# The last hidden pair of a Strassen MLP: its squared features stored raw and split later on POOL, first bank copies on VectorE

## The chip, the cores and the metric

The kernel runs on one NeuronCore of one Trainium2 chip. The metric is the device time of one execution in microseconds (us). TensorE (PE) multiplies; VectorE (DVE), ScalarE (ACT) and GpSimd (POOL) do the elementwise work; SyncE (SP) issues nearly all DMAs. SBUF is the on-chip memory, PSUM holds matmul results in eight banks of 128 partitions x 512 fp32, DRAM is off chip.

## What is computed

One layer of a diffusion backbone on 1024 latent tokens and 128 context tokens. Time mixing comes first (two thirds of the time); the change is in the MLP behind it:

```python
x = x + gate1 * rms_norm(y, lp['g_post_mix'])
h = rms_norm(x, lp['g_pre_mlp']) * (1.0 + scale2) + shift2
f = jnp.square(jax.nn.relu(jnp.einsum('btd,df->btf', h, lp['w_mlp1'])))   # 1024 -> 4096
f = jnp.einsum('btf,fd->btd', f, lp['w_mlp2'])                            # 4096 -> 1024
x = x + gate2 * rms_norm(f, lp['g_post_mlp'])
```

## The kernel before

Every fp32 operand of a matmul is split into a high and a low part (type F32R): ScalarE copies to the rounded type (high), VectorE or POOL subtracts that from the original (low). A product is three matmuls: high-high, high-low, low-high.

**First MLP matmul.** The 4096 hidden columns are 16 pairs p of 2 x 128. For p >= 2, `strassen(p, hooks)` (L2210) does a pair with Strassen's scheme, in eleven steps; after step s it calls the functions in `hooks[s]`, so these lists place all other work. `store` (L2112) puts the squared features in SBUF: `ft[0]` and `ft[1]`, one for each 128 hidden columns, hold 512 tokens in `[:, 0]`, 512 in `[:, 1]` and the last 128 in `[:, 2, 384:512]`. The second matmul uses Strassen too, with A11, A12, A21, A22 as the four 128x512 blocks of a pair. It needs seven split operands of a pair, A11, A12, A22 and the sums S1 to S4: `f_sum` (L2130) makes a sum on VectorE, `f_split` (L2138) splits one operand (one ScalarE copy, one VectorE subtraction, one store of 512 KB to the DRAM tensor `Fd[p]`), `c_split` (L2146) does the 128 last tokens (`Fc[p]`). A pair's operands are made during the next pair; the last pair (p = 15) has no next one, so its splits stand in a row behind `strassen`, ahead of the second matmul (the loop over `("A11", "S1", ...)`).

**Second MLP matmul.** `mlp2(g, hooks)` (L2384) runs for g = 0 to 7; group g covers pairs 2g and 2g + 1 (e = 0, 1). Group 7 is the only one that reads pair 15. A group starts with a context step for each half h of the output columns (banks `ps_s`, `ps_P`), then four passes u over `QUAD`, each of seven steps of six matmuls (`STEP2`): steps 0, 2, 4 and 6 share one bank (`ps_g`), step 1 has `ps_m`, steps 3 and 5 share `ps_G`. After each step `take` (L2346) brings the bank to the accumulator `acc` in SBUF, because the next step on the same bank needs it read first. In group 0 the two context takes and four of a pass's seven (steps 0, 2, 3 and 6, the first to reach their part of `acc`) copy the bank on ScalarE (L2348); all others add on VectorE (L2350).

**What surrounds it.** `f_load(g, u)` (L2330) loads a pass's split operands, 896 KB for each e, into the tiles `f` (`FT2`, four of them, u mod 2 by e), two passes ahead; `c_load` loads the context's. `group_hooks(g)` (L2420) lists, by (pass, step), the work for group g + 1: `w_load`/`w_half` load the W2 rows, `w_t` (L2311) makes the Strassen sums T1, T2, T4, T3 of W2 on POOL, `w_s` (L2317 copy on ScalarE, L2318 subtraction on POOL) splits B11 to B22 and the Ts. For group 0 the same is done on VectorE in the hooks of the last pair. The order is written by hand: each engine runs its instructions in the order in which the code emits them, and SP issues its DMAs so too, each waiting for its semaphores.

## Time and profile before

| | us |
|---|---|
| median of 3 runs | 1717.57 (1716.85 to 1719.27) |
| the profiled execution, its own time | 1720.59 |
| its span, first to last instruction | 1718.8 |
| PE busy in the span | 1586.3 (92%) |
| DVE, ACT, POOL busy | 1110.8, 803.7, 516.9 |

The profiled execution is 3.0 us above the median of the runs, and 1.8 us of it lie outside the span. The mean granted TensorE clock is 0.973 of full speed. In the rows below, a line of a timeline has start and duration (us), engine, line, operation, out<-in, the count, and in brackets the engine's idle time before it and what ended it. A line of busy time by stage has the stage, its length, then busy us and (xcount) of PE, PEld, DVE, ACT and POOL, the granted clock, the DMA engines' share and GB/s. A line of instructions by form has busy us and mean ns, and behind the bar the idle time before them. The stretch that the change touches begins with the last pair, at about 1299 us of the span, and ends with the groups of the second matmul.

### The profile page before, as it was taken

Reading aid. Unit: us, or ns where it says so; the run is one execution under the profiler, and the core shown is the slowest. Engines: PE = TensorE matmul, PEld = TensorE weight load, DVE = VectorE, ACT = ScalarE, POOL = GpSimd, SP = SyncE. Lnnn points to the kernel's source line nnn. Section 1 sums busy time; section 2 is a strip of 40 time slices with the busy share of each in tenths; the row PEclk is TensorE's granted clock in tenths of the full one; section 3 lists DMA queues with packets and bytes.
Section 4 is the critical chain, followed back from the end, with each engine's and each line's share of the span. In section 5 each row is a group of like instructions: output and inputs, shape, how many; then the busy total and the mean of one; then the engine's idle time right before and its main releaser. Section 6 shows DMA issues by size and latency. Waiting matters only on the chain.

```text
span 1718.8 us, 33152 instructions
## 1 busy us (share of the span) xinstructions
PE 1586.3 (92%) x13035; PEld 1337.5 (78%) x13035; DVE 1110.8 (65%) x1884; ACT 803.7 (47%) x1549; POOL 516.9 (30%) x593
## 2 busy tenths in 40 slices
PE   6799988898998999779998999999999699999996
PEld 2678777777887776657686999999999578888884
DVE  2835676576876887956648986677667334444458
ACT  3734443343425577635445666666666422222112
POOL 3100186758310210111220000000000387666635
PEclk9899999989999999989999999999999899999999
DMA  9544857674753767899943467766667755566667
GB/s 312 190 135 132 205 139 185 158 193 113 186 128 95 177 138 182 200 215 253 244 171 122 143 203 236 232 224 220 222 221 261 279 194 215 223 232 233 226 242 260
DMA packets 362556, 341.19 MB, mean 199 GB/s; under 512 B 104600, under 2 KB 322912, under 8 KB 362400
## 3 DMA queue, kind: packets, MB, share of 16 engines
q1 hardware_dynamic: 360288, 331.53, 63.8%
q0 software_dynamic: 2112, 7.55, 1.3%
q8 instruction: 102, 1.67, 0.4%
q14 instruction: 54, 0.44, 0.1%
HBM read 214.72 MB, written 124.29 MB: 197 GB/s over the span
## 4 chain that ended last, share of the span: by engine, by line
PE 63%; DVE 13%; DMA 9%; POOL 5%; ACT 4%; issue 3%; SPq 3%; DVEq 0%; POOLq 0%; ACTq 0%
PE ps_g L2405 9%; PE ps_g L2221 6%; PE ps_P L2221 6%; PE ps_G L2405 4%; PE ps_g L531 3%; PE ps_G L2221 3%; PE ps_g L532 3%; PE ps_g L533 3%; PE ps_g L1662 3%; PE ps_m L2405 2%; POOL ar L1028 2%; POOL ar L1024 2%; PE ps_m L2221 2%; PE ps_G L1503 2%; PE ps_m L1534 2%
## 5 line engine op out<-in xcount | busy, mean ns | idle before, releaser
L531 PE MATMUL ps_g<-hH,wH 128*128 128x384 f32 x552 | 209.5, 380 | 2.6 <-DVE hH L270 1.9
L532 PE MATMUL ps_g<-hL,wH 128*128 128x384 f32 x552 | 191.5, 347 | 6.4 <-DVE hL L484 6.2
L533 PE MATMUL ps_g<-hH,wL 128*128 128x384 f32 x552 | 190.3, 345 | 0.0
L2318 POOL TENSOR_TENSOR sL<-w2r,sL 128x512 fp32r<-128x512 f32 x8 | 10.4, 1305 | 451.5 <-ACT sL L2317 449.4
L2350 DVE TENSOR_TENSOR acc<-ps_g,acc 128x512 f32<-128x512 f32 x116 | 80.0, 691 | 94.1 <-PE ps_g L2405 76.6
L531 PEld LDWEIGHTS ps_g<-hH,wH 128*128 128x128 f32 x552 | 107.9, 196 | 18.0 <-issue 8.5
L2221 PE MATMUL ps_P<-h2H,ws 128*128 128x384 f32 x432 | 118.3, 334 | 0.0
L532 PEld LDWEIGHTS ps_g<-hL,wH 128*128 128x128 f32 x552 | 108.0, 196 | 10.5 <-DVE hL L484 9.1
L2405 PE MATMUL ps_g<-sH,fT 128*128 128x512 f32 x408 | 109.1, 399 | 2.2 <-DVE acc L2350 1.3
L533 PEld LDWEIGHTS ps_g<-hH,wL 128*128 128x128 f32 x552 | 107.6, 195 | 0.0
L2405 PEld LDWEIGHTS ps_g<-sH,fT 128*128 128x128 f32 x408 | 77.2, 190 | 22.4 <-DVE acc L2350 2.6
L1024 POOL TENSOR_TENSOR ar<-ar 128x252 f32<-128x252 f32 (+22 forms) x124 | 79.6, 642 | 44.0 <-DMA ar<-NAd 35.3
L2120 ACT ACTIVATE ft<-ft 128x384 f32<-128x384 f32 x138 | 72.4, 524 | 40.8 <-DVE ft L2119 37.8
L1028 POOL TENSOR_TENSOR ar<-ar 128x252 f32<-128x252 f32 (+22 forms) x124 | 87.5, 705 | 9.3
L2221 PEld LDWEIGHTS ps_P<-h2H,ws 128*128 128x128 f32 x432 | 78.8, 188 | 0.0
L2405 PE MATMUL ps_G<-sL,fT 128*128 128x512 f32 x252 | 70.7, 403 | 3.0 <-ACT acc L2348 2.9
L1539 DVE TENSOR_TENSOR SV<-ps_m,Dt 64x256 f32<-64x256 f32 x136 | 57.1, 421 | 23.6 <-PE ps_m L1534 20.7
L2221 PE MATMUL ps_P<-h2L,ws 128*128 128x384 f32 x216 | 72.2, 334 | 0.0
L2350 DVE TENSOR_TENSOR acc<-ps_G,acc 128x512 f32<-128x512 f32 x60 | 41.4, 690 | 38.0 <-PE ps_G L2405 38.0
L2317 ACT ACTIVATE sL<-tt 128x512 fp32r<-128x512 f32 x31 | 19.6, 632 | 96.0 <-POOL tt L2311 64.7
L2221 PE MATMUL ps_G<-oT,ws 128*128 128x384 f32 x336 | 63.9, 339 | 0.2 <-DVE ft L2119 0.2
L1503 PE MATMUL ps_G<-SV,r 128*32 128x64 f32 x1152 | 53.7, 228 | 10.7 <-DVE SV L1539 10.3
(526 smaller groups left out, 4175.1 us busy)
## 6 DMA issues: line engine op xcount, KB each, us to landing
fT<-Fd SPq DMA_DIRECT2D x64, 896.0 KB
Fd<-fs SPq DMA_DIRECT2D x108, 512.0 KB
KGd<-ar SPq DMA_DIRECT2D x96, 192.0 KB
r<-KGd SPq DMA_DIRECT2D x36, 512.0 KB
mw<-in_w_mod_dram SPq DMA_DIRECT2D x64, 256.0 KB
w1r<-in_w_mlp_dram SPq DMA_DIRECT2D x32, 512.0 KB
w2r<-in_w_mlp_dram SPq DMA_DIRECT2D x31, 512.0 KB
raw<-in_w_in_dram SPq DMA_DIRECT2D x26, 512.0 KB
```

The lines of the kernel that those rows point to most:

```text
L531: T.matmul(ps, wH[:, k, :], hH[b][:, k, :], start=(k == 0), stop=False)
L532: T.matmul(ps, wH[:, k, :], hL[b][:, k, :], start=False, stop=False)
L533: T.matmul(ps, wL[:, k, :], hH[b][:, k, :], start=False, stop=(k == 7))
L1024: E.tensor_tensor(out=t, in0=X[:, :, 0:m, j:j + 1].to_broadcast([128, 2, m, w]), in1=n[:, :, j % 8:j % 8 + 1, j + 1:32].to_broadcast([128, ...
L1028: E.tensor_tensor(out=X[:, :, 0:m, j + 1:32], in0=X[:, :, 0:m, j + 1:32], in1=t, op=ALU.subtract)
L1503: T.matmul(RU[n][r0:r0 + 32, 0, p, :], KRG[n][kq][:, e, p, kc, 0:32], SV[n][s % NSV][:, e, p, :], start=True, stop=True)
L1539: Q.add("V", cv(256), lambda e=e, ks=ks: V.tensor_tensor(out=SV[n][(s + 1) % NSV][ks, e], in0=x["S"][ks], in1=dv[ks], op=ALU.mult), r=[("S ...
L1662: T.matmul(z["ps"], y["t"][:, q // 2, k], wo_t[4 + k][q % 2][:, hs_], start=first, stop=last and stop)
L2120: S_ = lambda: [S.activation(out=f, in_=x, func=fn) for x, fn in ((src if add is None else f, AF.Relu), (f, AF.Square))]
L2221: T.matmul(ps[ch], w[:, qw, k], h[q][:, k, :], start=(new and k == n == 0), stop=(k == 3 and n == 2), skip_group_check=True)
L2350: V.tensor_tensor(out=acc_(i, h), in0=ps, in1=acc_(i, h), op=ALU.add)
L2405: T.matmul(ps[ch], f[:, OPI[fx], qf], w[:, qw], start=(new and e == n == 0), stop=(e == 1 and n == 2), skip_group_check=True)
```

## The change

Four things change.

1. The last pair's operands are no longer made behind `strassen`. Its four blocks and the two 128-column remainders go raw to new DRAM tensors `Ar`, `Cr` (six stores, 1152 KB in place of 3840 KB).
2. `later()` makes the operands during groups 1 to 4 (the table allows up to 5): raw blocks are loaded into three tiles `lr`, POOL makes the four sums, and 14 half operands (128x256) and two context tiles are split by a ScalarE copy and a POOL subtraction in the unused end of the `f` tiles (now 12 slots long, 9 before), then stored to `Fd[15]` and `Fc[15]`. `plan()` gives one piece to each of the eight places of `ROOM` in a group, with its store and loads two places later.
3. `take` copies on VectorE where it copied on ScalarE.
4. `f_load(0, 1)` is issued in two parts inside the last pair (hooks 8 and 10), and group 0's `w_load(1, 1)` moves into its hooks at (0, 0).

```diff
+    Ar = [[dr.tile([128, 512], F32, name=f"Ar{i}{b}") for b in range(2)] for i in range(2)]
+    Cr = [dr.tile([128, 128], F32, name=f"Cr{i}") for i in range(2)]
...
+    def raw(i, b):
+        SY.dma_start(out=Ar[i][b][:], in_=ft[i][:, b])
+
+    def later():
+        l0, l1, l2 = lr
+        rooms = itertools.cycle(range(4))
+        P = NP - 1
+        ld = lambda t, x: lambda: SY.dma_start(out=t, in_=Ar[int(x[2]) - 1][int(x[1]) - 1][:])
+        sums = lambda t, x, y, op: lambda: G.tensor_tensor(out=t, in0=x, in1=y, op=op)
+
+        def half(t, x, h):
+            def fn():
+                r = FT2[divmod(next(rooms), 2)][:, 9:11]
+                f = t[:, 256 * h:256 * h + 256].rearrange("p (u c) -> p u c", c=128)
+                S.activation(out=r[:, :, 0], in_=f, func=AF.Copy)
+                G.tensor_tensor(out=r[:, :, 1], in0=f, in1=r[:, :, 0].bitcast(F32), op=ALU.subtract)
+                return lambda: SY.dma_start(out=Fd[P][:, 2 * h:2 * h + 2, OPI[x]].bitcast(F32), in_=r.bitcast(F32))
+            return fn
...
+        return [(None, [ld(l0, "A21"), ld(l1, "A22"), ld(l2, "A11")]),
+                (half(l1, "A22", 0), []), (half(l1, "A22", 1), []), (sums(l0, l0, l1, ALU.add), [ld(l1, "A12")]),
+                (half(l0, "S1", 0), []), (half(l0, "S1", 1), []), (half(l2, "A11", 0), []), (half(l2, "A11", 1), []),
+                (sums(l0, l0, l2, ALU.subtract), []), (half(l0, "S2", 0), []), (half(l0, "S2", 1), []),
+                (half(l1, "A12", 0), []), (half(l1, "A12", 1), []), (sums(l0, l1, l0, ALU.subtract), ldc),
+                (half(l0, "S4", 0), []), (half(l0, "S4", 1), [ld(l0, "A21")]), (tile8(0), []), (tile8(1), []),
+                (sums(l2, l2, l0, ALU.subtract), []), (half(l2, "S3", 0), []), (half(l2, "S3", 1), [])]
+
+    ROOM = (("c", 1), (0, 1), (0, 6), (1, 3), (1, 5), (2, 0), (3, 0), (3, 5))
...
     def take(g, i, h, ps, first=False):
         if g == 0 and first:
-            S.activation(out=acc_(i, h), in_=ps, func=AF.Copy)
+            V.tensor_copy(out=acc_(i, h), in_=ps)
...
-        if g:
-            add(0, 2, lambda: w_load(n, 1))
+        add(0, 2 if g else 0, lambda: w_load(n, 1))
+        for k, fns in defer.pop(g, {}).items():
+            add(*k, *fns)
...
-                     5: [sp(0, "T2"), sp(0, "B21"), sp(0, "T1"), lambda: c_split(p, 0)],
+                     5: [sp(0, "T2"), sp(0, "B21"), sp(0, "T1"), lambda: raw(0, 0)],
...
-                     8: [rooms3, sp(1, "B12"), sp(1, "B22"), sp(0, "T4")],
+                     8: [rooms3, lambda: f_load1(0, 1, 0), lambda: raw(1, 1), sp(1, "B12"), sp(1, "B22"), sp(0, "T4")],
...
-                     10: [tt(1, "T1"), tt(1, "T2"), sp(1, "T2")]}
+                     10: [lambda: f_load1(0, 1, 1), lambda: raw(1, 0), tt(1, "T1"), tt(1, "T2"), sp(1, "T2")]}
...
-    rr = iter(R[2])
-    for x in ("A11", "S1", "A12", "S2", "A22", "S3", "S4"):
-        if x[0] == "S":
-            f_sum(x)
-        if x != "S1":
-            f_split(NP - 1, x, None if x[0] == "A" else next(rr))
-        if x == "S2":
-            f_split(NP - 1, "S1", next(rr))
-    c_split(NP - 1, 1)
-    f_load(0, 1)
+    raw(0, 1)
+    for i in range(2):
+        SY.dma_start(out=Cr[i][:], in_=ft[i][:, 2, BLK:512])
     pDp.close()
...
     w_half(1, 1)
-    w_load(1, 1)
+    lr = [mp["ac"].tile([128, 512], F32, name=f"lr{i}") for i in range(3)]
+    for i in (1, 4, 2, 5):
+        acc_(i, 0)
+    plan()
```

VectorE between the last weight split of group 0 and its first bank work, before (`fs`, `fS`, `sL`, `s`: pieces of the last pair; `ft`: its squared features; the numbers tell tiles of one name apart):

```order
L2318 TENSOR_TENSOR sH_14014<-tt,sH_14014 128x512
L2143 TENSOR_TENSOR fs<-ft_10157,fs 128x4x128
L2135 TENSOR_TENSOR fS_14078<-ft_10157,ft_10158 128x512
L2143 TENSOR_TENSOR fs<-ft_10158,fs 128x4x128
L2135 TENSOR_TENSOR fS_14084<-fS_14078,ft_10157 128x512
L2143 TENSOR_TENSOR sL_14015<-fS_14084,sL_14015 128x4x128
L2143 TENSOR_TENSOR sL_14015<-fS_14078,sL_14015 128x4x128
L2143 TENSOR_TENSOR fs<-ft_10158,fs 128x4x128
L2135 TENSOR_TENSOR fS_14096<-ft_10157 128x512
L2143 TENSOR_TENSOR s_13991<-fS_14096,s_13991 128x4x128
L2135 TENSOR_TENSOR fS_14084<-ft_10158,fS_14084 128x512
L2143 TENSOR_TENSOR s_13992<-fS_14084,s_13992 128x4x128
```

Behind these stand one `fc` subtraction and then the adds into `acc`. The same place now:

```order
L2385 TENSOR_TENSOR sH_14017<-tt,sH_14017 128x512
L2418 COPY acc_14092<-ps_s 128x512
L2418 COPY acc_14092<-ps_P 128x512
L2418 COPY acc_14093<-ps_g 128x512
L2420 TENSOR_TENSOR acc_14093<-ps_m,acc_14093 128x512
L2418 COPY acc_14094<-ps_g 128x512
L2418 COPY acc_14094<-ps_G 128x512
L2420 TENSOR_TENSOR acc_14094<-ps_g,acc_14094 128x512
```

All twelve instructions on the last pair, the `fc` among them, are gone from here, and three bank copies stand directly behind the last weight split. SP from the loads of group 0's first pass on, before (`fT<-Fd`: the f tiles; `Fd_10120` is pair 15's tensor, `Fd_10119` pair 14's):

```order
L2332 DMA fT_13969<-Fd_10106 128x1792
L2144 DMA Fd_10119<-fs 512x1x256
L2276 DMA w2r<-in_w_mlp_dram 128x1024
L2144 DMA Fd_10120<-fs 512x1x256 x2
L2144 DMA Fd_10120<-sL_14015 512x1x256 x2
L2144 DMA Fd_10120<-fs 512x1x256
L2144 DMA Fd_10120<-s_13991 512x1x256
L2144 DMA Fd_10120<-s_13992 512x1x256
L2151 DMA Fc_10136<-fc 128x256
L2332 DMA fT_14109<-Fd_10105 128x1792
L2332 DMA fT_14111<-Fd_10106 128x1792
L2276 DMA w2r_14122<-in_w_mlp_dram 128x1024
```

And now:

```order
L2398 DMA fT_13972<-Fd_10106 128x1792
L2398 DMA fT_14019<-Fd_10105 128x1792
L2157 DMA Ar_10140<-ft_10164 128x512
L2147 DMA Fd_10119<-fs 512x1x256
L2343 DMA w2r<-in_w_mlp_dram 128x1024
L2398 DMA fT_14066<-Fd_10106 128x1792
L2157 DMA Ar_10139<-ft_10164 128x512
L2157 DMA Ar_10138<-ft_10163 128x512
L2581 DMA Cr_10141<-ft_10163 128x128
L2581 DMA Cr_10142<-ft_10164 128x128
L2343 DMA w2r_14095<-in_w_mlp_dram 128x1024
```

The second pass's loads stood behind the eight stores and now stand ahead of the raw stores; the last is the second half of group 1's first weight load. POOL in group 1, around the split of T3 (e = 0) and T1 (e = 1), before and now:

```order
L2311 TENSOR_TENSOR tt<-w2r_14317,w2r 128x512
L2318 TENSOR_TENSOR sL_13866<-tt,sL_13866 128x512
L2318 TENSOR_TENSOR sH_14014<-w2r,sH_14014 128x512
L2318 TENSOR_TENSOR s_13989<-w2r,s_13989 128x512
L2318 TENSOR_TENSOR sL_14015<-w2r,sL_14015 128x512
L2318 TENSOR_TENSOR sH_13865<-w2r,sH_13865 128x512
L2311 TENSOR_TENSOR tt<-w2r 128x512
L2318 TENSOR_TENSOR sL_14015<-tt,sL_14015 128x512
```

```order
L2378 TENSOR_TENSOR tt<-w2r_14293,w2r 128x512
L2172 TENSOR_TENSOR fT_13970<-lr_14098,fT_13970 128x2x128
L2385 TENSOR_TENSOR sL_13872<-tt,sL_13872 128x512
L2172 TENSOR_TENSOR fT_13972<-lr_14098,fT_13972 128x2x128
L2385 TENSOR_TENSOR sH_14017<-w2r,sH_14017 128x512
L2385 TENSOR_TENSOR s_13992<-w2r,s_13992 128x512
L2385 TENSOR_TENSOR sL_14018<-w2r,sL_14018 128x512
L2385 TENSOR_TENSOR sH_13871<-w2r,sH_13871 128x512
L2378 TENSOR_TENSOR tt<-w2r 128x512
L2165 TENSOR_TENSOR lr_14097<-lr_14097,lr_14098 128x512
L2385 TENSOR_TENSOR sL_14018<-tt,sL_14018 128x512
```

Two halves (`fT<-lr`) and one sum (`lr<-lr`) stand between the weight instructions; such pieces follow through group 3.

## Rows read from the trace of the kernel before

**Rows 1.** busy time by stage: the last pair, group 0, group 1
```profile
1299.20:1324.06 24.86, 24.86 (x144) 24.86 (x144) 17.25 (x30) 18.23 (x37) 0.00 (x0) 1.00 0.80 272
...
1324.06:1388.94 64.88, 48.99 (x193) 37.60 (x193) 23.38 (x37) 26.79 (x49) 26.82 (x22) 0.89 0.71 262
...
1388.94:1433.65 44.71, 44.71 (x194) 36.07 (x193) 20.05 (x29) 9.71 (x17) 31.95 (x26) 1.00 0.60 224
```

**Rows 2.** timeline of TensorE in group 0, rows after pauses
```profile
1331.97 0.96 PE L2405 MATMUL ps_g<-s,fT 128*128 128x512 f32 x3 [1.46 <-DMA fT<-Fd]
...
1332.77 1.56 PE L2405 MATMUL ps_m<-s,fT 128*128 128x512 f32 x6
...
1344.21 1.65 PE L2405 MATMUL ps_g<-sL,fT 128*128 128x512 f32 x3 [9.88 <-ACT acc L2348]
...
1360.62 1.66 PE L2405 MATMUL ps_g<-sH,fT 128*128 128x512 f32 x6 [0.92 <-ACT acc L2348]
...
1386.04 0.97 PE L2405 MATMUL ps_G<-sL,fT 128*128 128x512 f32 x3 [1.30 <-ACT acc L2348]
```

**Rows 3.** timeline of VectorE around the start of group 0
```profile
1333.57 0.68 DVE L2318 TENSOR_TENSOR sH<-tt,sH 128x512 fp32r<-128x512 f32 x1
...
1334.17 0.68 DVE L2143 TENSOR_TENSOR fs<-ft,fs 128x512 fp32r<-128x512 f32 x1
...
1343.14 0.28 DVE L2150 TENSOR_TENSOR fc<-ft,fc 128x128 fp32r<-128x128 f32 x1
...
1344.19 0.69 DVE L2350 TENSOR_TENSOR acc<-ps_m,acc 128x512 f32<-128x512 f32 x1 [0.76 <-ACT acc L2348]
```

**Rows 4.** timeline of ScalarE: a bank copy, a weight copy
```profile
1343.56 0.60 ACT L2348 ACTIVATE acc<-ps_g 128x512 f32<-128x512 f32 x1
...
1362.73 0.63 ACT L2317 ACTIVATE sL<-tt 128x512 fp32r<-128x512 f32 x1 [2.16 <-POOL tt L2311]
```

**Rows 5.** timeline of TensorE, third step of group 1's first pass
```profile
1397.30 0.86 PE L2405 MATMUL ps_g<-sL,fT 128*128 128x512 f32 x3
```

**Rows 6.** busy time by stage around the pause and in group 0's rest
```profile
1336.40:1344.20 7.80, 0.00 (x0) 0.00 (x0) 4.95 (x10) 4.58 (x9) 0.00 (x0) 0.50 1.00 337
...
1344.20:1350.00 5.80, 5.79 (x14) 4.58 (x15) 0.68 (x1) 0.86 (x2) 0.00 (x0) 0.50 1.03 338
...
1350.00:1388.94 38.94, 34.38 (x144) 26.51 (x143) 7.61 (x11) 15.52 (x28) 26.82 (x22) 1.00 0.64 247
```

**Rows 7.** instructions by form: a VectorE copy from PSUM
```profile
L270 DVE COPY r<-ps_g 128x512 f32<-128x512 f32 x2 | 1.4, 692 | 0.7 <-PE ps_g L1662 0.7
```

**Rows 8.** timeline of TensorE, two other pauses of about 2 us
```profile
338.82 0.55 PE L981 MATMUL ps_G<-ident,ar 128*128 128x128 f32 x3 [1.90 <-DVE ar L963]
...
918.01 0.50 PE L1901 MATMUL ps_s<-woH,yH 128*128 128x512 f32 x1 [2.03 <-DVE ot L1913]
```

**Rows 9.** busy time by stage after those two pauses
```profile
340.00:343.00 3.00, 3.00 (x28) 2.19 (x28) 1.41 (x3) 0.98 (x2) 2.77 (x4) 0.50 0.64 149
...
914.00:920.00 6.00, 3.97 (x18) 2.94 (x17) 4.95 (x8) 2.55 (x6) 0.00 (x0) 1.00 0.66 201
```

**Rows 10.** timeline of POOL: its first weight split, then group 1
```profile
1350.93 1.30 POOL L2318 TENSOR_TENSOR sL<-w2r,sL 128x512 fp32r<-128x512 f32 x1 [449.39 <-ACT sL L2317]
...
1425.53 1.29 POOL L2318 TENSOR_TENSOR sL<-tt,sL 128x512 fp32r<-128x512 f32 x1 [7.56 <-ACT sL L2317]
...
1435.43 1.29 POOL L2318 TENSOR_TENSOR s<-tt,s 128x512 fp32r<-128x512 f32 x1 [0.74 <-ACT s L2317]
```

**Rows 11.** instructions by form: POOL with two inputs of 256 columns
```profile
L1028 POOL TENSOR_TENSOR ar<-ar 128x256 f32<-128x256 f32 x4 | 3.3, 824 | 0.3
...
L1024 POOL TENSOR_TENSOR ar<-ar 128x256 f32<-128x256 f32 x4 | 2.8, 694 | 0.2
```

**Rows 12.** SyncE timeline, the loads of a pass in group 3
```profile
1493.26 1.42 SPq L2332 DMA_DIRECT2D fT<-Fd  x2
```

**Rows 13.** busy time and DMA share later in that pass
```profile
1499.40:1503.20 3.80, 3.80 (x18) 3.07 (x17) 2.08 (x3) 1.17 (x3) 3.80 (x4) 1.00 0.01 6
```

More of the change, by code (lines that the diff above doesn't have):

```diff
@@ L2151, in c_split, with tile8, fn @@
         SY.dma_start(out=Fc[p][:, i].bitcast(F32), in_=t.bitcast(F32))
+    def raw(i, b):
[14 more added lines that the diff above has]
+            return fn
+        def tile8(i):
+            def fn():
+                r, f = FT2[i, 0][:, 11], l1[:, 128 * i:128 * i + 128]
+                S.activation(out=r[:, 0], in_=f, func=AF.Copy)
+                G.tensor_tensor(out=r[:, 1], in0=f, in1=r[:, 0].bitcast(F32), op=ALU.subtract)
+                return lambda: SY.dma_start(out=Fc[P][:, i].bitcast(F32), in_=r.bitcast(F32))
+            return fn
+        ldc = [lambda i=i: SY.dma_start(out=l1[:, 128 * i:128 * i + 128], in_=Cr[i][:]) for i in range(2)]
+        return [(None, [ld(l0, "A21"), ld(l1, "A22"), ld(l2, "A11")]),
[5 more added lines that the diff above has]
+                (sums(l2, l2, l0, ALU.subtract), []), (half(l2, "S3", 0), []), (half(l2, "S3", 1), [])]
@@ new lines, in hymba_kernel, with plan, go, f @@
+    ROOM = (("c", 1), (0, 1), (0, 6), (1, 3), (1, 5), (2, 0), (3, 0), (3, 5))
+    defer = {}
+    def plan():
+        at = [(g, k) for g in range(1, 6) for k in ROOM]
+        left = {}
+        def go(fn, j):
+            def f():
+                left[j] = fn() if fn else None
+            return f
+        for j, (fn, tr) in enumerate(later()):
+            n0 = j if j == 0 else j + 3
+            g, k = at[n0]
+            defer.setdefault(g, {}).setdefault(k, []).append(go(fn, j))
+            def out(j=j, tr=tr):
+                st_ = left.pop(j)
+                for t in tr:
+                    t()
+                if callable(st_):
+                    st_()
+            g, k = at[n0 + 2] if j else at[n0]
+            defer.setdefault(g, {}).setdefault(k, []).append(out)
```

6 lines of the change are left out of this document (4 added, 2 removed).

## The prediction

> **What bounds the kernel now.** I read the busy times by stage first. In the stage of the last pair and in every group of the second matmul from group 1 on, TensorE is busy all the time: group 1 takes 44.71 us and PE is busy 44.71 of them [rows 1]. Its 32 steps (four for the context, 28 in the passes) therefore take 44.71 / 32 = 1.397 us each, a pass of seven 9.78. Group 0 has the same matmuls and takes 64.88 us, of which PE is busy 48.99 [rows 1]. The excess is 64.88 - 44.71 = 20.2 us, and it is all that the change can win.
>
> The timeline of TensorE says what the excess is [rows 2]. PE waits 1.46 us for the first pass's second load (DMA). After step 1, which ends at 1332.77 + 1.56 = 1334.33, it waits 9.88 us for ScalarE's copy of the bank. Later there are four short waits for the same kind of copy, the first 0.92 and the last 1.30 us; together they are the idle time of the rest of the group, 38.94 - 34.38 = 4.6 us [rows 6]. That is 15.9 us. The other 4.3 are mostly the clock: the granted clock stands at 0.50 (1.2 GHz) from 1336.4 to 1350.0 [rows 6], so the 5.79 us that PE worked in its last part did the work of 2.9; the remainder is the start-up behind each wait.
>
> The timelines of the other engines give the causes. VectorE finishes group 0's last weight split at about 1334.2, and the last pair's work, eleven instructions and an `fc`, follows from 1334.17 to 1343.4 [rows 3]. ScalarE's copies for that work alternate with it, and its bank copies stand behind them: the third, on which step 2 depends, runs from 1343.56 to 1344.16, and PE starts at 1344.21, 0.05 us later [rows 2, 4]. The four short waits come from order too: a bank copy stands behind a ScalarE weight copy that waits about 2 us for POOL [rows 4].
>
> **The change part by part.** *The long wait.* VectorE's list is the same up to 1334.17, and then come three bank copies. A copy of this shape from PSUM took 692 ns [rows 7], and back-to-back instructions of this size start 0.60 apart (1333.57 to 1334.17) [rows 3]. So the third copy ends at 1334.17 + 2 x 0.60 + 0.69 = 1336.06, and step 2 starts 0.05 later, at 1336.1. Its bank was finished before step 1, so the copy itself waits for nothing new. From step 2 on a group has 26 steps: 26 x 1.397 = 36.3, as from 1397.30 to the end of group 1 at 1433.65 [rows 1, 5]. With 0.1 for the start-up (0.96 in place of the 0.86 that three matmuls take without a pause) [rows 2, 5], group 0 ends at 1336.1 + 36.3 + 0.1 = 1372.5 in place of 1388.94: **16.4 us** saved. The 1.46 us for the DMA remain, and lie inside this sum.
>
> *The short waits* are in that sum at nothing, because VectorE now has one bank operation per step, 0.69 of 1.397 us, and nothing else in group 0. If that cover were gone, they would cost up to their 4.6 us.
>
> *The clock.* A pause of 1336.1 - 1334.3 = 1.8 us stays. After a pause of 1.90 the clock stood at 0.50 in the next 3 us; after one of 2.03 it stayed at 1.00 [rows 8, 9]. So the rows allow both. At half clock 3.6 us of work do 1.8, thus the cost is 0 to 1.8 us. The two rows are equally near; I take the middle, **0.9**.
>
> *The earlier loads.* Two loads of 896 KB and raw stores now stand nearer to group 0's first loads in SP's order. If the DMA engines gave all of them an equal share, the first part of this, an 896 KB load and a 256 KB store (1.18 MB), would delay the load that PE already waits for by 1.18 / 0.337 = 3.5 us at the rate of the full DMA stretch [rows 6]. Step 0 would end at 1336.3, its copy at 1337.0, and step 1 at 1337.7, so step 2 would start 1.6 us later than above. The other end is 0, since they are issued behind that load. I take 0, by the row: in the run of before, too, later issues stood behind it, and the wait was 1.46 [rows 2].
>
> The Trainium skill, page "DMA: Bandwidth & Descriptors", section "Queues, rings and completion order", says that all DMAs issued by SP go through one ring on each DMA engine, consumed in ring order. By that rule the term is 0, and with sharing it would be 1.6; no run here shows which.
>
> *The moved work.* Removed from behind the last pair are twelve VectorE and eight ScalarE instructions and 3840 KB of stores, all of it priced in the long wait. Added in groups 1 to 3 are, on POOL, four sums of 512 columns at 1.30 [rows 10], 14 halves at 0.69 to 0.82 [rows 11] and two context tiles, at most the same: at the upper price 5.2 + 16 x 0.82 = 18.3 us. Group 3 gets most: two sums, four halves and two tiles, 2.6 + 4.9 = 7.5 us. In a group POOL stands idle 7.56 us in one piece before it splits T1 of e = 1, since ScalarE must wait there for a slot that PE still reads [rows 10]. So the worst group just fits. There is a reserve besides: the last split a group makes, T3, ends at 1435.43 + 1.29 = 1436.7, and PE needs it at step 3 of the next group's first pass, seven steps after 1433.65, at 1443.4, 6.7 us later [rows 1, 10]. ScalarE is busy 9.7 of 44.7 us [rows 1] and no longer touches a bank. I cost this at nothing.
>
> *SP and the DMA engines.* In groups 1 to 4 SP gets 16 stores and 7 loads more, none above 256 KB. A pass's loads were issued at 1493.26, and from 1499.4 the DMA engines stood idle at 0.01 of their time [rows 12, 13]; the next pass but one needs them one pass, 9.8 us, after their issue, at 1503.1, so 3.7 us are free. A piece of 256 KB in front of them is 0.8 us at 0.337 MB per us [rows 6]. Cost nothing; its other end is in the rivals.
>
> *Group 1's weights.* POOL has 24 instructions of 1.30 for them and up to eight waits of 0.74 [rows 10], 37 us. It must be through by step 3 of group 1's first pass, 1372.5 + 9.8 = 1382.3, so it must start by 1345. Before, it started at 1350.93, behind ScalarE's bank copies [rows 10]; if it could start no earlier, PE would wait 1350.9 + 37 - 1382.3 = 5.6 us. ScalarE is free from about 1334.2 now, and the first W2 rows were requested ahead of the last pair's work in SP's order. I take 0; the bound is 0 to 5.6.
>
> *Sum.* 16.4 - 0.9 = 15.5 us saved. The profiled execution, 1720.59 by its own time, would become 1705.1; it stands 3.0 us above the median of the runs, 1717.57, and I take the saving from the median: **1702.1**.
>
> **The rivals.** *POOL becomes the bound for a while.* In its fixed order it also meets pieces whose operand is still being loaded: the context tiles and the last sum, in group 3, each follow their load by one or two places. If every piece paid its own 0.74 us handshake with ScalarE, group 2 and group 3 would each add some 7.5 + 8 x 0.74 = 13.4 us against 7.56 free; 2 x 5.8 = 11.7, less the reserve of 6.7, leaves 5.0 us on the path; or group 1's weights come late, up to 5.6. Against it: most pieces stand in gaps in which POOL would wait for ScalarE anyway. It gives 1703 to 1709, about 1707.
>
> The Trainium skill, page "GPSIMD Engine Reference", section "Engine selection", puts elementwise work on VectorE, GpSimd being about twice as slow for two inputs. The trace agrees on the price (1.30 us against 0.68 for the same subtraction, [rows 3, 10]); by that rule alone this rival would be the forecast, but it leaves out POOL's idle 7.56 us.
>
> *SP's order turns against it: slower.* Each of the 16 stores waits on SP for its POOL piece, and the next pass's loads queue behind it. If POOL lags so that a store holds SP for more than the 3.7 us that are free, PE waits for the f tiles in every one of the 16 passes of groups 1 to 4. It takes (15.5 + 3.4) / 16 = 1.2 us per pass to end slower, so a lag of 4.9 us at every store: about 1722. Against it: a store stands two places, four to fourteen us of PE time, behind its piece, and POOL reaches its work ahead of PE.
>
> *It does not do what it says.* The bank copies stay late because VectorE, too, is held, by tiles of `acc` laid over ones whose stores have not landed, or because the first loads slip by far more than 3.5 us. For no gain PE would have to stand still until 1344 or the clock to fall again and again: about 1716. The first three copies write room last read by VectorE itself, which speaks against it.
>
> **How the numbers follow.** The forecast with its own terms (clock 0 to 1.8, loads 0 to 1.6, about a us either way between runs) has 0.78: 1700.5 to 1704.8, likeliest 1702.1. POOL as the bound has 0.11, slower through SP 0.05, no effect 0.06. A measurement of this kernel tells 0.2%, 3.4 us, from no change: below 1714.1 is faster. Forecast and first rival are both faster, 0.89; no effect is 0.06; slower 0.05. The range reaches from 1699.5 (clock kept, all loads in time, a fast run) to 1708.0 (most of the first rival), and leaves out some 0.15.
>
> **What would show it right or wrong.** Group 0 should take 48 to 51 us, with one pause of about 1.8 us and no wait on ScalarE; the three copies should end at about 1336; groups 1 to 6 should stay at 44.7 us each, with POOL's 7.56 us wait shrunk in groups 1 to 3. Wrong would be: a wait of PE for `fT` or for weight splits in groups 1 to 4, a first pause over 2.5 us, or a clock at 0.50 for more than 4 us behind it.

## The result

The changed kernel takes 1701.89 us (median of 4 runs, 1699.96 to 1707.3), the kernel before in the same runs 1718.42; the ratio of the two times is 0.9897, with a 95% interval of 0.9874 to 0.9919. It ran twice more, each time beside a fresh set of runs of before: 1704.61 against 1719.06 (ratio 0.9925, 0.9910 to 0.9941) and 1704.68 against 1719.94 (0.9921, 0.9905 to 0.9936). The saving is thus 16.5, 14.5 and 15.3 us. The forecast was 1702.1, by a saving of 15.5.

The profiled execution took 1701.36 us by its own time, its span 1699.6. Busy time by stage of the changed kernel (stage, length, then busy us and count of PE, PEld, DVE, ACT and POOL, granted clock, DMA share, GB/s), from the last pair through group 4:

```profile
1294.60:1319.45 24.85, 24.85 (x144) 24.85 (x144) 17.12 (x29) 18.03 (x36) 0.00 (x0) 1.00 0.82 282
1319.45:1369.55 50.10, 46.60 (x194) 37.18 (x193) 27.79 (x42) 13.60 (x25) 28.24 (x23) 0.97 0.74 280
1369.55:1414.25 44.70, 44.70 (x193) 36.07 (x192) 20.75 (x30) 9.96 (x18) 33.23 (x28) 1.00 0.68 253
1414.25:1458.98 44.73, 44.73 (x194) 36.07 (x193) 20.75 (x30) 11.71 (x23) 36.68 (x33) 1.00 0.76 265
1458.98:1503.77 44.79, 44.79 (x194) 36.09 (x192) 20.74 (x30) 11.19 (x22) 36.76 (x33) 1.00 0.72 261
1503.77:1548.47 44.70, 44.70 (x193) 36.07 (x192) 20.75 (x30) 9.65 (x17) 31.28 (x26) 1.00 0.64 235
```

The second line answers to the 64.88 us of [rows 1]: group 0 is 14.8 us shorter, and TensorE stands idle for 50.10 - 46.60 = 3.50 us in it, in place of 15.9. Groups 1 to 4 are full of TensorE work as before, although POOL now does the pieces in groups 1 to 3.

The two spans differ by 19.2 us, more than group 0 gives. Another 4.6 come from ahead of the change, and 0.2 are lost behind it: group 0 starts at 1319.45 here and at 1324.06 in [rows 1], with the same code up to the last pair. In all profiles of this case that start lies between 1315.52 and 1325.26. So ends of executions are compared below only through medians, and profiles through the length of a stage, or through times counted from the start of group 0.

TensorE's timeline of group 0 (start, duration, engine, line, operation, out<-in, count, in brackets the idle time before it and what ended it) has one pause, in the first pass. Before, the group had six, the DMA wait, the long wait and the four short ones, of which [rows 2] show four:

```profile
1325.04 1.56 PE L2475 MATMUL ps_g<-s,fT 128*128 128x512 f32 x6
1326.44 1.56 PE L2475 MATMUL ps_m<-s,fT 128*128 128x512 f32 x6
1331.50 0.96 PE L2475 MATMUL ps_g<-sL,fT 128*128 128x512 f32 x3 [3.50 <-DVE acc L2418]
```

VectorE's timeline shows what it waits for: the last weight split of group 0, and then the three bank copies, 0.60 us apart, in place of the last pair's split that stood at 1334.17 in [rows 3].

```profile
1328.97 0.69 DVE L2385 TENSOR_TENSOR sH<-tt,sH 128x512 fp32r<-128x512 f32 x1
1329.57 0.68 DVE L2418 COPY acc<-ps_s 128x512 f32<-128x512 f32 x1
1330.17 0.68 DVE L2418 COPY acc<-ps_P 128x512 f32<-128x512 f32 x1
1330.77 0.68 DVE L2418 COPY acc<-ps_g 128x512 f32<-128x512 f32 x1
```

The third copy ends at 1331.45, and TensorE starts at 1331.50. After the pause the granted clock fell to 0.50, for about 3.5 us instead of the 13.6 of [rows 6], 7.8 of which TensorE stood still (busy time by stage, columns as above; the granted clock is the third number from the right):

```profile
1331.50:1333.00 1.50, 1.50 (x6) 1.25 (x7) 0.69 (x1) 0.09 (x1) 1.50 (x2) 0.97 1.01 379
1333.00:1335.00 2.00, 2.00 (x6) 1.55 (x5) 0.69 (x1) 0.00 (x0) 0.67 (x1) 0.50 1.06 420
1335.00:1337.30 2.30, 2.30 (x8) 1.85 (x8) 0.69 (x1) 1.15 (x2) 1.05 (x1) 0.72 0.87 354
1337.30:1340.00 2.70, 2.70 (x13) 2.16 (x13) 1.38 (x2) 0.00 (x0) 2.70 (x3) 1.00 0.01 3
```

POOL's timeline answers to [rows 10]. It starts group 1's weights at 1331.15, 11.7 us after the start of group 0 (26.9 before), and its one long wait of each group, before 7.56 us in group 1 and 8.8 to 8.9 in groups 2 to 4, has become shorter in groups 1 to 3 (the rows at 1406.13, 1450.86 and, with a second wait at a context tile, 1481.94 and 1495.64), and is nearly whole again in group 4 (8.22):

```profile
1331.15 1.28 POOL L2385 TENSOR_TENSOR sL<-w2r,sL 128x512 fp32r<-128x512 f32 x1 [435.61 <-ACT sL L2384]
...
1406.13 1.29 POOL L2385 TENSOR_TENSOR sL<-tt,sL 128x512 fp32r<-128x512 f32 x1 [6.85 <-ACT sL L2384]
...
1450.86 1.29 POOL L2385 TENSOR_TENSOR sH<-tt,sH 128x512 fp32r<-128x512 f32 x1 [4.91 <-ACT sH L2384]
...
1481.94 0.46 POOL L2180 TENSOR_TENSOR fT<-lr,fT 128x128 fp32r<-128x128 f32 x1 [4.34 <-ACT fT L2179]
...
1495.64 1.30 POOL L2385 TENSOR_TENSOR s<-tt,s 128x512 fp32r<-128x512 f32 x1 [0.30 <-ACT s L2384]
...
1540.36 1.30 POOL L2385 TENSOR_TENSOR sL<-tt,sL 128x512 fp32r<-128x512 f32 x1 [8.22 <-ACT sL L2384]
```

### The profile page after: what moved, and what is told of

Its sections match the earlier page's. It is cut to its first block, busy times and chain, and to the rows that moved or that the text cites. A ratio compares the mean times of both kernels' runs of the same rounds, so it can differ in the third digit from the quotient of the medians.

```text
span 1699.6 us, 33202 instructions
## 1 busy us (share of the span) xinstructions
PE 1581.5 (93%) x13035; PEld 1336.8 (79%) x13035; DVE 1111.8 (65%) x1889; ACT 795.4 (47%) x1538; POOL 533.8 (31%) x613
## 4 chain that ended last, share of the span: by engine, by line
PE 64%; DVE 13%; DMA 7%; POOL 7%; ACT 4%; issue 3%; SPq 2%; DVEq 0%; POOLq 0%; ACTq 0%
PE ps_g L2475 10%; PE ps_g L2288 6%; PE ps_P L2288 6%; PE ps_G L2475 5%; POOL ar L1028 3%; PE ps_g L531 3%; PE ps_G L2288 3%; POOL ar L1024 3%; PE ps_g L532 3%; PE ps_g L533 3%; PE ps_m L2475 3%; PE ps_g L1662 2%; PE ps_m L2288 2%; PE ps_G L1503 2%; PE ps_m L1534 2%
## 5 line engine op out<-in xcount | busy, mean ns | idle before, releaser
L1539 DVE TENSOR_TENSOR SV<-ps_m,Dt 64x256 f32<-64x256 f32 x136 | 57.0, 420 | 20.9 <-PE ps_m L1534 15.2
```

What stands on the lines that cost most here:

```text
L1539: Q.add("V", cv(256), lambda e=e, ks=ks: V.tensor_tensor(out=SV[n][(s + 1) % NSV][ks, e], in0=x["S"][ks], in1=dv[ks], op=ALU.mult), r=[("S ...
```

## The experiments

Four questions were open: what each part of the change is worth alone, why the pause is 3.50 us and what the clock costs behind it, whether the moved work is really free, and whether the rest of group 0's excess can be had.

### Each part alone

**e1: the copies back on ScalarE.**

```diff
-            V.tensor_copy(out=acc_(i, h), in_=ps)
+            S.activation(out=acc_(i, h), in_=ps, func=AF.Copy)
```

> The changed kernel with its bank copies given back to ScalarE; the deferral stays. Theory A (both parts of the change are needed: the deferral for the long wait, the copies on VectorE for the four short ones): the long wait stays small, ScalarE is free from 1328.84 and its third copy ends near 1330.5, so TensorE restarts near 1330.6 instead of 1331.5; but the short waits behind ScalarE's weight copies return with up to 4.6 us, group 0 takes 50 to 54 us, median 1702 to 1706. Rival B (the deferral alone carries the gain, because it also lets POOL start group 1's weights 20 us earlier, so that ScalarE's weight copies no longer wait for POOL in front of a bank copy): no short wait, a first pause of 2.6 us, group 0 at 48 to 49.5 us, median 1700 to 1702, not above the changed kernel.

Measured: 1706.25 us median (1705.05 to 1707.2), ratio to before 0.9909 (0.9881 to 0.9938), 0.25 us above theory A's range. Group 0 runs from 1322.53 to 1375.30, 52.77 us. TensorE's timeline, the rows after a pause:

```profile
1333.42 0.97 PE L2475 MATMUL ps_g<-sL,fT 128*128 128x512 f32 x3 [1.98 <-ACT acc L2418]
...
1346.94 1.66 PE L2475 MATMUL ps_g<-sH,fT 128*128 128x512 f32 x6 [0.65 <-ACT acc L2418]
...
1350.21 0.96 PE L2475 MATMUL ps_G<-sL,fT 128*128 128x512 f32 x3 [1.60 <-ACT acc L2418]
...
1356.80 0.96 PE L2475 MATMUL ps_g<-sL,fT 128*128 128x512 f32 x3 [0.73 <-ACT acc L2418]
...
1372.39 0.97 PE L2475 MATMUL ps_G<-sL,fT 128*128 128x512 f32 x3 [1.32 <-ACT acc L2418]
```

ScalarE's timeline around the second of these pauses:

```profile
1345.77 0.63 ACT L2384 ACTIVATE sH<-tt 128x512 fp32r<-128x512 f32 x1 [2.92 <-POOL tt L2378]
1346.31 0.58 ACT L2418 ACTIVATE acc<-ps_g 128x512 f32<-128x512 f32 x1
```

The first pause is shorter than with VectorE, since ScalarE is free earlier: TensorE restarts 10.89 us after the start of group 0, not 12.05. But the four short waits are back, 4.30 us together: a weight copy waits 2.92 us for POOL, the bank copy stands behind it, and TensorE behind that. POOL's earlier start did not cure this, so rival B falls: the short waits come from the order on ScalarE, as theory A had it.

**e2: the copies alone, without the deferral.** The kernel before, with the same line in `take` on VectorE.

```diff
-            S.activation(out=acc_(i, h), in_=ps, func=AF.Copy)
+            V.tensor_copy(out=acc_(i, h), in_=ps)
```

> The kernel before with the bank copies on VectorE and nothing else changed. Theory A (the wait is for VectorE's and ScalarE's work for the last pair, which a change of engine does not pass): VectorE is busy with that work to 1343.4 in the profile of before, so the third copy ends near 1345.3, 1.1 us later than ScalarE's; the short waits of 4.6 us vanish; group 0 takes 61 to 62 us instead of 64.9, median about 1715. Rival B (short waits are POOL's lateness, not the order on ScalarE): TensorE then waits for the weight splits of group 1 instead, in group 1, and the sum is unchanged: 1717 to 1720.

Measured: 1715.45 us median (1711.69 to 1721.0), ratio 0.9970 (0.9948 to 0.9993). Group 0 takes 60.34 us (1320.29 to 1380.63), 0.7 less than theory A's range, and has a single wait on a copy; group 1 stays at 44.70, so rival B falls here too. That one pause of TensorE, and VectorE's last piece for the last pair with the third copy behind it:

```profile
1341.52 1.65 PE L2405 MATMUL ps_g<-sL,fT 128*128 128x512 f32 x3 [10.73 <-DVE acc L2348]
```

```profile
1339.38 0.29 DVE L2150 TENSOR_TENSOR fc<-ft,fc 128x128 fp32r<-128x128 f32 x1
...
1340.78 0.68 DVE L2348 COPY acc<-ps_g 128x512 f32<-128x512 f32 x1
```

The restart lies 21.23 us after the start of group 0; on ScalarE it was 1344.21 - 1324.06 = 20.15 [rows 1, 2]. The copies alone therefore make the long wait 1.08 us worse and take the short ones away, for 4.5 us in group 0. The deferral alone (e1) gives 64.88 - 52.77 = 12.1. Together they would be 16.6; the change gave 14.8, and the difference is mostly the clock, which held in e1 and fell behind the changed kernel's longer pause (1.5 us, see e3).

### The pause and the clock

**e3: the loads of pass 1 where they stood before.**

```diff
-                     8: [rooms3, lambda: f_load1(0, 1, 0), lambda: raw(1, 1), ...
+                     8: [rooms3, lambda: raw(1, 1), ...
-                     10: [lambda: f_load1(0, 1, 1), lambda: raw(1, 0), ...
+                     10: [lambda: raw(1, 0), ...
     for i in range(2):
         SY.dma_start(out=Cr[i][:], in_=ft[i][:, 2, BLK:512])
+    f_load(0, 1)
     pDp.close()
```

> The changed kernel with the loads of pass 1 issued after the raw stores, where they stood before, instead of ahead of them. Theory A (the 1.46 us for the first pass's load vanished because fewer bytes stand ahead of that load in SP's order, and the loads of pass 1 have 9 us to spare): no wait of TensorE for fT at the first pass, group 0 within 0.5 us of 50.1, same time as the changed kernel, 1700 to 1703. Rival (the earlier issue of pass 1's loads is part of the gain): a wait for fT of 1 us or more at pass 1, or the 1.46 us at pass 0 again; group 0 51 to 54 us.

Measured: 1700.3 us median (1699.64 to 1706.37), ratio 0.9885 (0.9856 to 0.9914); group 0 takes 48.56 us, without a wait for `fT` at pass 1. TensorE's timeline, and the clock behind the restart:

```profile
1326.80 0.97 PE L2475 MATMUL ps_g<-s,fT 128*128 128x512 f32 x3 [0.66 <-DMA fT<-Fd]
...
1331.74 0.97 PE L2475 MATMUL ps_g<-sL,fT 128*128 128x512 f32 x3 [2.57 <-DVE acc L2418]
```

```profile
1333.00:1335.00 2.00, 2.00 (x10) 1.62 (x9) 0.84 (x2) 0.00 (x0) 0.19 (x1) 1.00 0.99 410
```

The restart is at 1331.74 - 1319.69 = 12.05 us, the same as in the changed kernel, although TensorE here waited 0.66 us for a load first. So the DMA wait is not a term of the sum: VectorE's copies set the restart, and a wait ahead of it only shortens the pause. The clock held here, and from the restart to the end of group 0 it took 36.51 us; the changed kernel, with its fall, took 1369.55 - 1331.50 = 38.05. The fall cost 1.5 us there. Theory A was right on pass 1 and wrong in two signs: the first pass's load was waited for, and group 0 is 1.5 us shorter than 50.1. Its reason for the shorter load wait, fewer bytes ahead, doesn't hold either: ahead of that load a store of 128 KB has given way to one of 256 KB, issued earlier. Why the wait shrank from 1.46 us stays open.

**a2, a3: the changed kernel again.**

> The changed kernel once more, unaltered, as the partner of the runs beside it. In its first profile TensorE paused 3.50 us and the granted clock then stood at 0.50 for about 3.5 us; with the loads of pass 1 issued later, where TensorE restarted at the same place (12.05 us after the start of group 0), the pause was 2.57 us behind a short wait for fT, and the clock stayed at 1.00. Theory A (the clock's answer to a pause of this size varies, and is worth about 1.6 us): TensorE restarts 12.0 to 12.1 us after the start of group 0; group 0 takes 50.1 us with the fall or 48.5 without. Rival (the order of pass 1's loads decides): group 0 at 50.1 with a pause of 3.5 again. Median 1700 to 1703.

> The changed kernel a third time, the partner of the run beside it. It restarts 12.0 to 12.1 us after group 0's start, behind a pause of 2.4 to 3.5 us; group 0 takes 48.5 us where the clock holds and 50 to 51 where it falls. Median 1701 to 1705.

Measured: 1704.61 us median (1702.32 to 1707.41) and 1704.68 (1703.36 to 1707.12); group 0 took 50.96 and 50.09 us. The restart came 12.03 and 12.04 us after its start. In a2 the clock was low for longer than in the first profile; its pause, and the busy time behind it:

```profile
1332.50 1.65 PE L2475 MATMUL ps_g<-sL,fT 128*128 128x512 f32 x3 [3.48 <-DVE acc L2418]
```

```profile
1332.50:1334.00 1.50, 1.50 (x4) 1.21 (x5) 0.69 (x1) 0.84 (x2) 1.10 (x1) 0.50 1.03 395
1334.00:1336.00 2.00, 2.00 (x6) 1.60 (x5) 0.54 (x1) 0.00 (x0) 1.41 (x2) 0.50 1.07 419
1336.00:1338.00 2.00, 2.00 (x6) 1.53 (x5) 0.15 (x1) 0.72 (x2) 0.01 (x1) 0.53 0.91 371
```

From the restart it took 1371.43 - 1332.50 = 38.93 us, 2.4 more than in e3. The median of a2 lies 1.6 us above the range expected for it. Its rival, the order of pass 1's loads, isn't what sets the pause: e7 below has the changed kernel's order and paused 2.46 us, behind a load's 0.75.

**e5: the pause filled.** Thirteen matmuls into a bank that nobody reads stand behind step 1.

```diff
+                if (g, u, s_) == (0, 0, 1):
+                    fill = bank("G")
+                    for n in range(13):
+                        T.matmul(fill, fo(0, 0)[:, 7, 0], w2[0, 0, "B11"][:, 0], start=(n == 0), stop=(n == 12))
                 run(hooks, (u, s_))
```

> The changed kernel with 13 further matmuls of 512 columns behind step 1 of group 0's first pass, into a bank that nobody reads: 13 x 0.233 = 3.0 us of the 3.50 us pause are filled, while the bank copies and all else stay. Theory A (the clock fell because TensorE stood still): a pause of 0.5 us is left, the restart stays 12.0 to 12.2 us after the start of group 0, the granted clock stays at 1.00, group 0 takes 48.3 to 48.7 us. Rival D (the clock's fall has another cause): clock at 0.50 behind it for about 3.5 us, group 0 at 50.1. Rival E (the fillers themselves cost): restart later than 12.5, group 0 above 49.

Measured: 1699.23 us median (1695.71 to 1702.04), 5.4 below the changed kernel of the same runs (a2); group 0 took 48.54 us. TensorE's timeline, where the filler is line 2481 and the restart the row behind it, and the busy time after that:

```profile
1324.50 3.20 PE L2481 MATMUL ps_G<-s,fT 128*128 128x512 f32 x13
1327.56 0.97 PE L2475 MATMUL ps_g<-sL,fT 128*128 128x512 f32 x3
```

```profile
1329.00:1331.00 2.00, 2.00 (x10) 1.59 (x10) 1.03 (x2) 0.00 (x0) 2.00 (x2) 1.00 1.05 410
```

The restart is at 1327.56 - 1315.52 = 12.04 us behind the start of group 0, as in the changed kernel, although TensorE waited 0.32 us for a load in the first step, and the clock is at 1.00 all through. With the same copies, the same restart and 13 useless matmuls more, group 0 is 1.6 us shorter than in the first profile and 2.4 shorter than in a2. That the clock falls because TensorE stands still, and what the fall costs, is shown by this one profile, and the three of e6 below, with hardly a pause and the clock at 1.00, agree. (5.4 us between the medians is more than the clock's 1.5 to 2.4. In the two profiles the start of group 0 is at 1315.52 here and at 1320.47 in a2, with the same code before it; a spread of that kind, ahead of the filler, would cover the rest.)

Which pauses the clock passes over isn't settled by these runs. It held behind 1.98 (e1) and 2.57 us (e3) and fell behind 3.48 to 3.50 (five profiles) and behind 2.46 in e7, below.

### The moved work

**e7: without the deferred work.** `plan()` isn't called, and group 7 takes pair 14's features for pair 15's as well.

```diff
-    plan()
-        SY.dma_start(out=fo(u, e)[:, 0:7].bitcast(F32), in_=Fd[2 * g + e][:, u].bitcast(F32))
+        SY.dma_start(out=fo(u, e)[:, 0:7].bitcast(F32), in_=Fd[min(2 * g + e, NP - 2)][:, u].bitcast(F32))
```

> The changed kernel without the deferred work: no loads of the raw features, no sums, splits and stores of the last pair in groups 1 to 5; group 7 loads the features of the pair before in their place, so its output is another. Theory A (the deferred work is hidden): groups 1 to 6 take 44.7 us each as with it, POOL waits about 7.6 us before the split of T1 in groups 1 to 3 again, and the time is that of the changed kernel within 1 us (beyond the clock's 1.6 us in group 0). Rival (the deferral costs through DMA and SP without showing as a wait): 1.5 us or more below the changed kernel, outside group 0.

Measured: 1705.95 us median (1701.6 to 1710.01), against 1704.61 in the same runs with the work; the rival's gain of 1.5 us or more isn't there. Groups 1 to 3 take 44.68, 44.73 and 44.79 us, the same to 0.02. In POOL's timeline the long wait is 8.76 us in group 1, 8.75 in group 2, and in group 3:

```profile
1497.60 1.30 POOL L2385 TENSOR_TENSOR s<-tt,s 128x512 fp32r<-128x512 f32 x1 [8.85 <-ACT s L2384]
```

So the pieces took 1.9, 3.8 and 8.5 us out of long waits that POOL had anyway (in group 3, 4.34 of them only moved, to the wait at the context tile). POOL is busy 2.6, 6.0 and 6.1 us less here; the rest of the pieces' time came out of its waits of 0.74 us for ScalarE. The pause in this run, 2.46 us behind a load's 0.75, was followed by a fall of the clock, and group 0 took 50.09. TensorE's timeline and the busy time behind it:

```profile
1333.48 0.97 PE L2475 MATMUL ps_g<-sL,fT 128*128 128x512 f32 x3 [2.46 <-DVE acc L2418]
```

```profile
1335.00:1337.00 2.00, 2.00 (x6) 1.61 (x5) 0.69 (x1) 0.37 (x1) 2.00 (x2) 0.50 1.05 421
```

**e4: every half three times.**

```diff
                 G.tensor_tensor(out=r[:, :, 1], in0=f, in1=r[:, :, 0].bitcast(F32), op=ALU.subtract)
+                G.tensor_tensor(out=r[:, :, 1], in0=f, in1=r[:, :, 0].bitcast(F32), op=ALU.subtract)
+                G.tensor_tensor(out=r[:, :, 1], in0=f, in1=r[:, :, 0].bitcast(F32), op=ALU.subtract)
```

This is the subtraction of the 14 halves. The two context tiles' stays single, though the expectation counts it three times; without it the expectation's prices give 9.8 us more in group 2 and 5.6, not 7.2, in group 3.

> The changed kernel with each of the last pair's 16 split subtractions on POOL made three times over (same operands, same result): 1.4 us more for a half, 0.8 for a context tile, so 9.8 more in group 2 (seven halves) and 7.2 in group 3 (four halves, two tiles). In the changed kernel POOL waited 4.91 us before the split of T1 in group 2, and 4.34 + 0.30 in group 3. Theory A (POOL's lateness reaches TensorE only when it passes those waits and then a reserve of 6.7 us between its last split and the step that needs it): the lag is 4.9 at the end of group 2 and 4.9 + 7.2 - 4.6 = 7.5 in group 3; TensorE waits about 0.8 us, 0 to 2, for a weight split in group 3 or 4, and groups 1 to 6 together stay below 270.5 us (268.5 now). Rival F (no reserve: what passes the waits is on the path): about 7.5 us of waits, groups 2 to 4 longer by that. Rival G (SP's order: a store waits for a late piece and holds the loads behind it): TensorE waits for fT, 1 us or more per pass, in groups 2 to 4.

Measured, in one execution: 1704.57 us. Groups 1 to 3 take 44.68 to 44.79 us as before, group 4 takes 45.42 (1506.50 to 1551.92). TensorE's only pause in groups 1 to 6:

```profile
1517.81 0.73 PE L2477 MATMUL ps_G<-s,fT 128*128 128x512 f32 x2 [0.45 <-POOL s L2387]
```

That is theory A's mechanism: of the 16.3 us that eleven halves add to POOL in groups 2 and 3 (two more subtractions of 0.74 us each), 0.45 us reach TensorE as a wait, and group 4 is 0.7 longer. That its number came out too is partly luck. With the tiles left out theory A gives a lag of 4.9 + 5.6 - 4.6 = 5.9 us, less than its reserve of 6.7, and thus no wait. The measured lag is 8.2 us: POOL's last split of group 3 ends 11.25 us after the start of group 4, and 3.09 in the changed kernel. Repeated subtractions start 0.82 apart, not 0.74. The reserve, too, is larger, about 7.5 us, since the row shows only the last two of the step's six matmuls waiting, and the prediction counted to the step's start. Rival F's 7.5 us and rival G's waits for `fT` didn't appear. POOL as the bound, the prediction's first rival, begins just here, at about three times the halves' price.

**e8: the pieces on VectorE.** `G.tensor_tensor` becomes `V.tensor_tensor` in the three places of `later()`.

> The changed kernel with the last pair's deferred sums and split subtractions on VectorE instead of POOL; stores, loads and ScalarE's copies stay. VectorE is busy 20.8 of 44.7 us per group with one bank operation per step of 1.397 us, and has 0.71 us between two. Theory A (the pieces are hidden on either engine, and what counts is only that they left group 0): a sum of 0.69 fits between two bank operations, groups 1 to 6 stay at 44.7 us, POOL's wait before T1 is 8.7 us again. Rival H (VectorE in its order stands in front of TensorE: a piece that waits for ScalarE's copy or for a load holds the bank operation behind it): TensorE waits for VectorE in groups 1 to 3, at 21 places by 0.1 to 1 us or more, and they grow by 2 to 15 us together.

Measured, in one execution: 1708.08 us, with the start of group 0 at 1325.26, the latest of all, so the total says little. Busy time of groups 1 to 3:

```profile
1375.33:1420.02 44.69, 44.69 (x193) 36.07 (x192) 23.38 (x33) 9.96 (x18) 30.73 (x24) 1.00 0.69 253
1420.02:1464.86 44.84, 44.84 (x193) 35.99 (x192) 27.11 (x38) 11.49 (x23) 31.71 (x26) 1.00 0.77 264
1464.86:1509.91 45.05, 45.05 (x193) 36.01 (x192) 25.61 (x38) 11.11 (x22) 31.84 (x25) 1.00 0.73 260
```

Against 44.70, 44.73 and 44.79 that is 0.4 us more in all three together. Theory A is nearly right on the time, and rival H has a trace of truth. POOL's wait before T1 was whole only in group 1, 8.64 us; in groups 2 and 3 it was 5.07 and 1.97, behind new waits for ScalarE of 2.24 to 4.54 us. So the gain doesn't hang on POOL as the place of the pieces, only on their leaving group 0. POOL is the better place by 0.4 us, in one profile.

### The rest of the excess

**e6, three times: the first three copies on ScalarE, ahead of the T3 and T4 splits.** ScalarE stood idle for 2.30 us just then, waiting for VectorE. Its row in the changed kernel:

```profile
1327.69 0.63 ACT L2384 ACTIVATE sL<-tt 128x512 fp32r<-128x512 f32 x1 [2.30 <-DVE tt L2378]
```

```diff
-        if g == 0 and first:
+        if g == 0 and first and len(acc_done) < 3:
+            acc_done.append(i)
+            S.activation(out=acc_(i, h), in_=ps, func=AF.Copy)
+        elif g == 0 and first:
             V.tensor_copy(out=acc_(i, h), in_=ps)
...
+        if g == 0:
+            add(0, 0, lambda: w_s(0, 1, "T3", V), lambda: w_s(0, 1, "T4", V))
...
-    w_s(0, 1, "T3", V)
-    w_s(0, 1, "T4", V)
```

> The changed kernel with the first three bank copies (both of the context and that of step 0) on ScalarE, in the 2.3 us in which it stands idle from 1325.4, and the splits of T3 and T4 issued behind them; the other copies stay on VectorE. Theory A (the 3.50 us pause that is left is VectorE's last weight work ahead of the copies, and the clock fell because of that pause): step 0's copy ends near 1327.2, the pause is below 0.5 us, the granted clock stays at 1.00, group 0 takes 45 to 46 us, which is 4 to 5 less, median 1696.5 to 1698. Rival C (something else arrives just behind the copies: the loads of pass 1, ScalarE's T3 and T4 splits, the W2 rows for group 1): the pause goes down but a new wait for fT or for a weight split appears in passes 0 and 1 or in group 1, and group 0 with group 1 gains less than 2.5 us. Rival D (the clock falls anyway at this place): pause below 0.5 us but a granted clock at 0.50 for about 3 us, group 0 about 47.

> The version with the first three bank copies on ScalarE once more, beside the changed kernel, to weigh the two times: theory A says group 0 takes 45.5 to 46.5 us and the median lies 2.5 to 4.5 us below that of the changed kernel of the same runs; the rival, that the gain is lost elsewhere, says the medians agree within 1 us.

> The version with the first three bank copies on ScalarE a third time. Group 0 took 45.8 and 45.7 us in its two profiles, against 50.1 and 51.0; theory A: 45.5 to 46.5 again, and the median 2 to 5 us below the changed kernel beside it, so that all runs together set the two apart. Rival: the spread from run to run, which the start of group 0 shows (1315.5 to 1324.6 in kernels with the same code up to there), covers it, and the medians stay within 2 us.

Measured: group 0 takes 45.82, 45.69 and 45.69 us. The medians are 1702.35 (ratio to before 0.9891, 0.9861 to 0.9920), 1702.36 (0.9908, 0.9890 to 0.9926) and 1700.45 (0.9893, 0.9873 to 0.9914). The second and third stand beside a2 and a3, 2.3 and 4.2 us below them. All runs together have medians of 1702.2 (16 runs) and 1704.7 (15 of the changed kernel). So the stage came as theory A said and the total didn't: the first median was expected at 1696.5 to 1698, the second 2.5 us or more below a2. Behind group 0 the three profiles took 329.5 to 331.5 us to their end and the changed kernel's three 329.8 to 330.6, so they show no place where 4.4 us of group 0 would shrink to 2.5 between the medians; the spread ahead of group 0 may cover it. The third profile's group 0 with group 1, the pause that is left, and ScalarE's third copy:

```profile
1318.44:1364.13 45.69, 45.29 (x194) 35.93 (x193) 25.80 (x39) 14.43 (x26) 25.96 (x21) 1.00 0.81 307
1364.13:1408.82 44.69, 44.69 (x194) 36.07 (x193) 20.75 (x30) 10.47 (x19) 35.57 (x30) 1.00 0.69 252
```

```profile
1327.38 0.97 PE L2479 MATMUL ps_g<-sL,fT 128*128 128x512 f32 x3 [0.40 <-ACT acc L2420]
```

```profile
1326.73 0.60 ACT L2420 ACTIVATE acc<-ps_g 128x512 f32<-128x512 f32 x1 [1.38 <-DVE tt L2378]
```

The pause falls from 3.5 to 0.40 us and the clock stays at 1.00. No new wait comes in passes 0 and 1 or in group 1 (the 0.75 us for a load in the first profile is within what other runs have), so rivals C and D fall. This is the fastest of the versions in its group 0, 1.0 us above a full group. What is left there is a copy that waits for VectorE's last subtraction for T3: the accumulator presumably lies on room which that one still reads; that wasn't tried.

## Why the prediction was right

The bound was named rightly, and the largest term to a hundredth: the restart was predicted at 1336.1, which is 12.04 us behind the start of group 0 at 1324.06, and it came 12.03 to 12.05 us behind it in all profiles of the changed kernel. Step by step:

- **The long wait** (16.4): right. The copies stood where the count of VectorE's instructions put them, 0.60 apart. From the restart to the end of group 0 the sum had 36.4 us; with the clock up it took 36.51 (e3).
- **The 1.46 us for the DMA** were expected to remain. The changed kernel's first profile has none, and of the others with the new order of loads, three show 0.32 to 0.75 us. The prediction held that they lie inside the sum, and so it is: without them TensorE reached the pause earlier and waited longer. That is why the pause was 3.50 and not 1.8 us. Why the load came earlier isn't shown. "A first pause over 2.5 us" was given as a sign of error; the sign was badly chosen, since it is the restart, not the pause, that the sum rests on.
- **The short waits** (4.6, inside the sum): right. e2 loses them by the copies alone, e1 gets 4.30 back without.
- **The clock** (0.9, bounds 0 to 1.8): this term was mis-sized. The fall cost 1.5 us in the first profile and 2.4 in a2. The upper bound took 3.6 us at half clock behind a pause of 1.8, a time that no row of the prediction gives ([rows 9] show 3.0 us at 0.50). The pause was twice as long, since the DMA wait had vanished, and the clock stayed low for about 3.5 us, in a2 for 5.4 behind the restart. That the longer pause made the fall dearer isn't shown: e7's 2.46 us cost the same 1.5. Group 0 was thus forecast at 48.4 + 0.9 = 49.3 us and took 50.1 (once 51.0). The sign of error named for it, a clock at 0.50 for more than 4 us, was met in a2.
- **The earlier loads** (0 of 0 to 1.6): right as to the sum; moving them back (e3) changed neither the restart nor pass 1. By the ring order that the Trainium skill gives ("DMA: Bandwidth & Descriptors", section "Queues, rings and completion order") what is issued behind the first pass's load would cost it nothing. The runs agree as far as they go: with the loads moved back the wait was 0.66, with them ahead it was between 0 and 0.75.
- **The moved work** (0): right, and shown by taking it out (e7). The count of 7.5 us for the worst group was near: 36.76 - 30.65 = 6.1 us of POOL's busy time in group 3. The 7.56 us of idle time that it was to fit into is group 1's; in groups 2 and 3 there were 8.8 to 8.9. The reserve was about 7.5 us in place of 6.7 (e4).
- **SP and the DMA engines** (0) and **group 1's weights** (0): right. No wait for `fT` or a weight split appears in groups 1 to 6, and POOL started group 1's weights 15.2 us sooner, counted from the start of group 0.

Of the rivals, POOL as the bound needed the pieces to pay one handshake each; most paid none, because ScalarE's copy was long done when POOL came to them. SP's order never turned: no load of groups 1 to 6 was late, not even with every half three times over. In group 7, which alone reads pair 15, TensorE waits for `fT` in both kernels, 1.23 and 0.19 us before, 1.23 and 0.61 now. The total came out at 1701.89 for 1702.1 with some luck: group 0 gave 0.8 us less than forecast with its clock term, and the median of the first four runs is 2.7 below those of a2 and a3, whose savings are 14.5 and 15.3.

## What to carry to other kernels

When a stalled stage is to be emptied, count the instructions that will stand in front of the releasing one on its engine: that gives the restart, and a pause is only the restart less the time of arrival, so a gain ahead of it makes the pause longer, and behind a pause the clock may fall. Look next for an engine that is idle at just that moment (here ScalarE, 2.30 us) and put the first releasing instructions there, even if the steady state belongs elsewhere: three copies moved that way were worth 4.4 us of group 0, 1.5 of them the clock's. Work moved into a full stage was free here as long as it fitted into the waits of its engine and the reserve behind them; measure the reserve by multiplying the work, not only by taking it away.
